# Stick-breaking attention: a backward running sum along the keys in place of products with triangles of ones

## The chip, the cores and the metric

One core of one Trainium2 chip runs the whole program. The metric is device microseconds for one execution. Of the engines, TensorE (PE in the profile, PEld for its weight loads) multiplies, VectorE (DVE) and ScalarE (ACT) work elementwise, GpSimd (POOL) and SyncE (SP) here mostly start transfers.

## What is computed

One layer of a hybrid encoder trunk on 512 frames of width 2048, in float32: RMSNorm, one wide projection, three attention branches A, B and C of 4 heads of width 128 each, SiLU gates, an up-projection per branch, sigmoid merge gates, an output projection and the residual. The change concerns branch C, stick-breaking attention. Cut to what matters, per head and block of 128 queries:

```python
z = q @ k.T * scale                                   # causal blocks of keys
mask = key < query                                    # strictly causal
lk = where(mask, log_sigmoid(-z), 0.0)
r = sum of lk over the keys from this one to the last # a suffix sum along the keys
a = where(mask, exp(z + r), 0.0)
out = a @ v
```

The reference writes the suffix sum as a product with a triangle of ones inside each block of 128 keys, plus the totals of the later blocks.

## The kernel before

**Number format.** Matrix products run in fp32r. To keep float32 accuracy every operand is split into a high part (ScalarE copies it to fp32r, L243) and a low part (VectorE subtracts, L247), and a product is made of high x high, high x low and low x high (`mm3`, L257 to L259).

**Weights.** Nearly all of TensorE's work is the weight products at L262. The weights come in units of 128 x 1024; ScalarE makes `wh`, VectorE makes `wl`, two units ahead of TensorE. From the second half of the start-up on, two output columns are made together by a scheme of seven products (`PairTask`, in the order 1, 2, 6, 5, 7, 3, 4). Each of the seven is a unit of 16 products on TensorE: 8 of 512 columns with `wh`, 8 of 256 columns with `wl`. Between the units VectorE and ScalarE take results out of PSUM and combine them (L703 to L759), and VectorE adds weight tiles (L641, L647).

**Heads.** The twelve heads run in the order C0 to C3, B0 to B3, A0 to A3, each beside the weight products of later columns. Their products use four PSUM tiles `att`; the weight products use others (`acc`). A stick-breaking head (class `Head`, `n == C`) does this:

- `plain` splits q and k.
- `stick_scores(j)`, for the key block j, makes the scores with the keys of the block as rows and the queries from that block on as columns: 512, 384, 256 or 128 columns. ScalarE takes them out (`z`), VectorE and ScalarE make log(1 + exp(z)) in `lk` (L1073 to L1079), VectorE sets it to zero on and above the diagonal (L1080, `m01`), and it is split into `lkh` and `lkl`.
- `stick_sums(j)` sums over keys, which lie on the partitions, on TensorE: for the block j a product with the triangle `nu_r`, for each later block a product with the full matrix `nones_r`, both for the high and the low part (L1096), and a product that adds the mask (L1098). VectorE adds `z` (L1107), ScalarE takes Exp (L1110), and the result, which has the keys on the partitions already, is split into `ah` and `al`.
- `v_trans` transposes v (L1123), `av` multiplies (L1162 to L1164), and `silu` makes the gate.

A softmax head (A, B) has its scores the other way round, queries on the partitions, and turns the weights at the end by transposes (L1025):

```python
def soft_trans(self, j):
    for i in range(QB):
        yield self.event("s", i)
    yield from self.parts_of(j)
    yield atts, 1
    yield PE, 0.11 * (QB - j)
    ps = att()
    for i in range(j, QB):
        nc.tensor.transpose(ps[:, blk(i)], self.p[i][:, blk(j)], identf)
    if self.nth("t", QB):
        give(t2s, 3)
    yield from split(*self.hl[j], ps[:, j * P:], S - j * P, self.event("a", j))
    give(atts)
```

**What sets the order.** Each piece of work is a generator that yields what it waits for (events, free slots of tiles) and which engine it will use for how long by a formula in the code. `Flow` plays these through on three clocks, for TensorE, ScalarE and VectorE, takes the piece that can start first (then the one due first), and calls it; the order in which the pieces are called is the order of the instructions on these three engines. On the chip each engine then works through its own list in order, and waits where an operand is not there. A head's pieces are started at set units (`OFF`: scores from the head's unit + `cs`, sums from + `ct`), and wait for what they need. Slots: 21 tiles of 128 x 512 (`t2s`) for everything, 4 PSUM tiles `att`.

Of the kernel before, what the change touches and what calls it, by code (L numbers as in the profile page):

```python
# [161 lines left out]
def hybrid_kernel(  # L162
# [50 lines left out]
    def blk(i):  # L213
        return slice(i * P, (i + 1) * P)
# [67 lines left out]
    def stored(slots, n, kb):  # L282
# [30 lines left out]

    nc.gpsimd.affine_select(out=nu_f, in_=onef, pattern=[[-1, P]], base=0, channel_multiplier=1,
                            compare_op=ALU.is_ge, fill=0.0)
# [569 lines left out]
    class Head:  # L885
        def __init__(self, n, h, last=False):
            self.n, self.h, self.last = n, h, last
            self.prev = heads[-1] if heads else None
            heads.append(self)
            self.hl, self.z, self.lk = [None] * QB, [None] * QB, [None] * QB  # L890
            self.summed, self.lk_given = [False] * QB, []
            self.c, self.ev, self.count = {}, {}, {}
# [137 lines left out]

        def tile_of(self, key, j, dt=F32):

            self.tiles = getattr(self, "tiles", {})
            if (key, j) not in self.tiles:
                t = t2(key, dt)
                self.tiles[key, j] = t[:, :S - j * P]
                if j in (1, 3):
                    self.tiles[key, 1], self.tiles[key, 3] = t[:, :S - P], t[:, S - P:]
            return self.tiles[key, j]

        def turn(self):
# [4 lines left out]

        def room_of(self, key, j, n):
            if j in (1, 3):
                if (key, 4 - j) in self.count:
                    return  # L1050
            self.count[key, j] = 1
            yield t2s, n

        def stick_scores(self, j):
            n = S - j * P
            for e in (("p", Q), ("p", K)):
                yield self.event(*e)
            yield from self.room_of("z", j, 1)
            yield atts, 1
            (qh, ql), (kh, kl) = self.c[Q], self.c[K]  # L1060
            yield PE, mm_us(n, 3)
            ps = att()[:, j * P:]
# [3 lines left out]
            z = self.z[j] = self.tile_of("z", j)  # L1066
            yield ACT, act_us(n)
            nc.scalar.activation(z, ps, AF.Copy, scale=SCALE)
            give(atts)
            yield t2s, 1  # L1070
            t = t2("lk")[:, j * P:]
            yield DVE, dve_us(n)
            nc.vector.scalar_tensor_tensor(t, z, -1.0, z, op0=ALU.mult, op1=ALU.min)  # L1073
            yield ACT, act_us(n)
            nc.scalar.activation(t, t, AF.Exp)
            yield ACT, act_us(n)
            nc.scalar.activation(t, t, AF.Ln, bias=1.0)
            yield DVE, dve_us(n) + dve_us(P)
            nc.vector.scalar_tensor_tensor(t, z, 0.0, t, op0=ALU.max, op1=ALU.add)  # L1079
            nc.vector.tensor_mul(t[:, :P], t[:, :P], m01)  # L1080
            yield from self.room_of("lk", j, 2)
            self.lk[j] = self.tile_of("lkh", j, F32R), self.tile_of("lkl", j, F32R)
            yield from split(*self.lk[j], t, n, self.event("s", j))
            give(t2s)

        def stick_sums(self, j):
            n = S - j * P
            for i in range(QB):
                yield self.event("s", i)
            yield from self.parts_of(j)  # L1090
            yield atts, 1
            yield PE, sum(mm_us(S - i * P, 2) for i in range(j, QB)) + mm_us(P)
            ps = att()
            for i in range(j, QB):
                for part in self.lk[i]:
                    nc.tensor.matmul(ps[:, i * P:], nu_r if i == j else nones_r, part,  # L1096
                                     start=i == j and part is self.lk[j][0], stop=False)
            nc.tensor.matmul(ps[:, blk(j)], identb, mskc, start=False, stop=True)  # L1098

            self.summed[j] = True  # L1100
            for k, need in ((0, (0,)), (2, (0, 1, 2)), (1, (0, 1, 2, 3))):
                if k not in self.lk_given and all(self.summed[i] for i in need):
                    self.lk_given.append(k)
                    give(t2s, 2)
            a = self.z[j]
            yield DVE, dve_us(n)
            nc.vector.tensor_add(a, a, ps[:, j * P:])  # L1107
            give(atts)
            yield ACT, act_us(n)
            nc.scalar.activation(a, a, AF.Exp)  # L1110
            yield from split(*self.hl[j], a, n, self.event("a", j))
            if self.nth("z", QB):
                give(t2s, 3)

# [61 lines left out]
        def stages(self):  # L1176

            s, t = (OFF["s1"], OFF["t1"]) if self.last else (OFF["s"], OFF["t"])
            v, o = (OFF["v1"], OFF["av1"]) if self.last else (OFF["v"], OFF["av"])
            one = lambda fn, i: lambda: fn(i)  # L1180
            if self.n == C:
                g = [(0, one(self.plain, K)), (0, one(self.plain, Q))]
# [453 lines left out]
```

## Time and profile before

| | |
|---|---|
| Time, three runs | 1356.82, 1358.31, 1358.43 us; median 1358.31 |
| Span of the profiled execution | 1356.7 us |
| Busy: PE, PEld, DVE, ACT, POOL | 98%, 85%, 81%, 59%, 7% of the span |
| Transfers | 262 MB, 193 GB/s on average |
| First products with triangles, last ones | start at 147.4 us, 353.8 us |
| Chain that ended last | 96% PE, of it 82% the products `acc` at L262, 0.8% L1096 |

The profiled execution's own time is not listed beside the three runs; its span is 0.1 us below the quickest of them. A busy share says how much of the time an engine had an instruction in work; matmuls overlap each other, so the share of PE is read together with its list of waits.

### The profile page before, as it was taken

To read this page: it belongs to the slowest core of one execution; us is meant where nothing else is said; L and a number is where in the kernel's file an instruction comes from. 1 tells how busy PE (TensorE), PEld (TensorE's weight loads), DVE (VectorE), ACT (ScalarE), POOL (GpSimd) and SP (SyncE) were. 2 spreads that over 40 slices of the span, in tenths; PEclk is the share of its full clock that TensorE was granted. 3 is DMA by queue.
4 is the path that set the end of the run, shared out by engine and by line. 5 is a ranking of instruction groups with operands and counts; after the bars stand their busy time and mean duration, and the time that the engine had idled before them with its cause. 6 is when DMAs were issued, how large, how long until landed. Compare 5 with 4: busy or idle time off the path is not lost.

```text
span 1356.7 us, 19786 instructions
## 1 busy us (share of the span) xinstructions
PE 1334.7 (98%) x7394; PEld 1157.1 (85%) x7394; DVE 1105.1 (81%) x1592; ACT 802.8 (59%) x1240; POOL 94.2 (7%) x125
## 2 busy tenths in 40 slices
PE   7999999999999999999999999999999999989998
PEld 5788888888888888888888888888888788878887
DVE  5898997978878788787888878778787877888786
ACT  6655765646565566655667556665566655454443
POOL 0000000000100001000010000100000000000100
PEclk9999999999999999999999999999999999989999
DMA  9555667677677777777767777677767755748893
GB/s 328 170 145 151 178 163 197 169 209 192 173 189 204 196 205 172 193 198 200 201 171 196 186 193 201 168 186 199 184 182 248 252 187 181 209 127 246 237 243 95
DMA packets 91056, 262.01 MB, mean 193 GB/s; under 512 B 10168, under 2 KB 16440, under 8 KB 90960
## 3 DMA queue, kind: packets, MB, share of 16 engines
q1 hardware_dynamic: 72384, 201.96, 44.5%
q0 software_dynamic: 14976, 54.53, 24.3%
q10 hardware_dynamic: 3600, 4.26, 0.9%
q8 instruction: 58, 0.95, 0.3%
q14 instruction: 38, 0.31, 0.1%
HBM read 241.03 MB, written 19.69 MB: 192 GB/s over the span
## 4 chain that ended last, share of the span: by engine, by line
PE 96%; DVE 2%; DMA 0%; issue 0%; ACT 0%; SPq 0%; DVEq 0%; ACTq 0%
PE acc L262 82%; PE att L262 8%; DVE wl L247 1%; PE att L1096 1%; PE att L1025 1%; DVE m L247 1%; PE att L1164 1%; PE att L1163 1%; PE att L258 1%; PE att L259 1%; PE att L257 1%; PE att L1162 1%; DMA x<-in_xT 0%; PE att L1123 0%; PE att L923 0%
## 5 line engine op out<-in xcount | busy, mean ns | idle before, releaser
L247 DVE TENSOR_TENSOR wl<-raw,wh 128x1024 fp32r<-128x1024 f32 (+1 forms) x412 | 493.6, 1199 | 156.6 <-ACT wh L243 153.7
L243 ACT ACTIVATE wh<-raw 128x1024 fp32r<-128x1024 f32 (+1 forms) x412 | 427.2, 1038 | 148.6 <-PE acc L262 68.6
L262 PE MATMUL acc<-x,wh 128*128 128x512 f32 x1600 | 417.5, 396 | 9.9 <-ACT wh L243 9.9
L262 PEld LDWEIGHTS acc<-x,wh 128*128 128x128 f32 x1600 | 286.5, 189 | 61.6 <-ACT wh L243 9.9
L262 PE MATMUL acc<-t,wh 128*128 128x512 f32 x1056 | 273.7, 395 | 0.0
L262 PEld LDWEIGHTS acc<-x,wl 128*128 128x128 f32 x1504 | 210.5, 190 | 18.9
L262 PE MATMUL acc<-x,wl 128*128 128x256 f32 (+1 forms) x1504 | 223.6, 289 | 0.0
L262 PEld LDWEIGHTS acc<-t,wh 128*128 128x128 f32 x1056 | 187.5, 189 | 31.3
L262 PEld LDWEIGHTS acc<-t,wl 128*128 128x128 f32 x1056 | 145.1, 190 | 11.1
L262 PE MATMUL acc<-t,wl 128*128 128x256 f32 x1056 | 148.6, 282 | 0.0
L278 POOL DMA_DIRECT2D raw<-in_w_col x88 | 76.0, 864 | 941.0 <-DMA raw<-in_w_col 482.4
L262 PE MATMUL acc<-m,wh 128*128 128x512 f32 x448 | 114.4, 398 | 6.4 <-DVE m L247 6.0
L262 PEld LDWEIGHTS acc<-m,wh 128*128 128x128 f32 x448 | 81.8, 192 | 21.8 <-DVE m L247 6.4
L757 ACT ACTIVATE c<-acc 128x256 f32<-128x256 f32 x50 | 19.2, 383 | 104.2 <-PE acc L262 99.2
L735 ACT ACTIVATE u<-acc 128x512 f32<-128x512 f32 x50 | 29.8, 597 | 73.3 <-PE acc L262 73.3
L262 PE MATMUL att<-y,wh 128*128 128x512 f32 x256 | 66.6, 391 | 1.3 <-DVE y L247 1.3
L262 PEld LDWEIGHTS acc<-m,wl 128*128 128x128 f32 x448 | 62.1, 193 | 5.2 <-DVE wl L247 0.8
L262 PE MATMUL acc<-m,wl 128*128 128x256 f32 x448 | 63.4, 285 | 0.4 <-DVE wl L247 0.4
L641 DVE TENSOR_TENSOR raw<-raw,raw 128x1024 f32<-128x1024 f32 x52 | 63.4, 1219 | 0.4
L647 DVE TENSOR_TENSOR raw<-raw,raw 128x1024 f32<-128x1024 f32 x52 | 63.3, 1218 | 0.3
L718 ACT ACTIVATE v<-acc 128x512 f32<-128x512 f32 x52 | 31.1, 598 | 49.4 <-PE acc L262 46.1
L262 PEld LDWEIGHTS att<-y,wh 128*128 128x128 f32 x256 | 47.9, 188 | 12.2 <-DVE y L247 2.4
(211 smaller groups left out, 1408.9 us busy)
## 6 DMA issues: line engine op xcount, KB each, us to landing
raw<-in_w_col SPq DMA_DIRECT2D x236, 512.0 KB, 4.3
raw<-in_w_col POOLq DMA_DIRECT2D x88, 512.0 KB, 6.1
raw<-in_w_out SPq DMA_DIRECT2D x40, 512.0 KB, 4.5
gl<-c SPq DMA_DIRECT2D x48, 256.0 KB, 2.6
raw<-in_w_up SPq DMA_DIRECT2D x32, 384.0 KB, 3.2
sg<-gl SPq DMA_DIRECT2D x48, 256.0 KB, 4.7
raw<-in_w_out POOLq DMA_DIRECT2D x16, 512.0 KB, 6.2
x<-in_xT SPq DMA_DIRECT2D x16, 256.0 KB, 7.0
```

The lines of the kernel that those rows point to most:

```text
L243: nc.scalar.activation(hi, src, AF.Copy)
L247: nc.vector.tensor_sub(lo, src, f(hi))
L257: nc.tensor.matmul(ps, lh, rh, start=start, stop=False, skip_group_check=more)
L258: nc.tensor.matmul(ps, lh, rl, start=False, stop=False, skip_group_check=more)
L259: nc.tensor.matmul(ps, ll, rh, start=False, stop=stop, skip_group_check=more)
L262: nc.tensor.matmul(ps, w, x, start=start, stop=stop, skip_group_check=more)
L278: nc.gpsimd.dma_start(to, src, accum_op=ALU.add)
L641: nc.vector.tensor_add(w[1], w[1], w[5])
L647: nc.vector.tensor_add(w[2], w[2], w[1])
L718: nc.scalar.activation(self.v, ps, AF.Copy)
L735: nc.scalar.activation(self.u, ps, AF.Copy)
L757: nc.scalar.activation(c, ps[:, RH], AF.Copy, scale=-1.0)
```

## The change

The scores of a stick-breaking head are made with the queries on the partitions, as in a softmax head, so that the keys lie along the row. The mask is added to the scores of the diagonal block (VectorE). log(1 + exp(z)) is made as before. The sum over the later keys is one instruction of VectorE a block of queries, a running sum that starts at the row's end and goes backwards (all operands are `t[:, ::-1]`; the second operation, a maximum with the same values, leaves the sum as it is, since all terms are at least zero). VectorE subtracts it from z, ScalarE takes Exp, and the weights are turned by `soft_trans` and split as in a softmax head. The split of the log terms into high and low parts, the 20 products with triangles and full matrices and the 4 mask products of each head are gone, and with them three constants. A new first piece, `stick_start`, takes three tiles for z after the head before has its own; nine were taken piece by piece before (three for z, six for the split log terms). The diff, cut to its core:

```diff
-    nones_r = cp.tile([P, P], F32R, name="nones_r")
-    nc.vector.tensor_scalar_mul(nones_r, onef, -1.0)
...
-    nu_r = cp.tile([P, P], F32R, name="nu_r")
-    nc.vector.tensor_scalar_mul(nu_r, nu_f, -1.0)
...
-    m01 = cp.tile([P, P], F32, name="m01")
-    nc.gpsimd.affine_select(out=m01, in_=onef, pattern=[[1, P]], base=0, channel_multiplier=-1,
-                            compare_op=ALU.is_gt, fill=0.0)
-    mskc = cp.tile([P, P], BF16, name="mskc")
-    nc.gpsimd.affine_select(out=zerof, in_=zerof, pattern=[[1, P]], base=0, channel_multiplier=-1,
+    mskc = cp.tile([P, P], F32, name="mskc")
+    nc.gpsimd.affine_select(out=mskc, in_=zerof, pattern=[[-1, P]], base=0, channel_multiplier=1,
                             compare_op=ALU.is_gt, fill=NEG)
-    nc.vector.tensor_copy(mskc, zerof)
...
-        def stick_scores(self, j):
-            n = S - j * P
-            for e in (("p", Q), ("p", K)):
+        def stick_start(self):
+            yield from self.turn()
+            yield t2s, 3
+            self.p = tri("p")[::-1]
+            set_(self.event("room"))
+
+        def stick_scores(self, i):
+            m = (i + 1) * P
+            for e in (("p", Q), ("p", K), ("room",)):
                 yield self.event(*e)
-            yield from self.room_of("z", j, 1)
             yield atts, 1
             (qh, ql), (kh, kl) = self.c[Q], self.c[K]
...
-            mm3(ps, kh[:, blk(j)], kl[:, blk(j)], qh[:, j * P:], ql[:, j * P:], True, True)
+            mm3(ps, qh[:, blk(i)], ql[:, blk(i)], kh[:, :m], kl[:, :m], True, True)
...
+            yield DVE, dve_us(P)
+            nc.vector.tensor_add(z[:, blk(i)], z[:, blk(i)], mskc)
...
             nc.vector.scalar_tensor_tensor(t, z, 0.0, t, op0=ALU.max, op1=ALU.add)
-            nc.vector.tensor_mul(t[:, :P], t[:, :P], m01)
-            yield from self.room_of("lk", j, 2)
-            self.lk[j] = self.tile_of("lkh", j, F32R), self.tile_of("lkl", j, F32R)
-            yield from split(*self.lk[j], t, n, self.event("s", j))
+            yield DVE, dve_us(2 * m)
+            back = t[:, ::-1]
+            nc.vector.tensor_tensor_scan(back, back, back, 0.0, op0=ALU.add, op1=ALU.max)
+            yield DVE, dve_us(m)
+            nc.vector.tensor_sub(z, z, t)
             give(t2s)
-
-        def stick_sums(self, j):
...
+            yield ACT, act_us(m)
+            nc.scalar.activation(z, z, AF.Exp)
+            set_(self.event("s", i))
...
-                g += [(OFF["cs"] + i, one(self.stick_scores, QB - 1 - i)) for i in range(QB)]
-                g += [(OFF["ct"] + i, one(self.stick_sums, i)) for i in range(QB)]
+                g = [(0, one(self.plain, K)), (0, one(self.plain, Q)), (OFF["cs"] - 1, self.stick_start)]
+                g += [(OFF["cs"] + i, one(self.stick_scores, i)) for i in range(QB)]
+                g += [(OFF["ct"] + i, one(self.soft_trans, i)) for i in range(QB)]
```

**Where the instructions stand now.** TensorE, the fourth stick-breaking head (C3). Before, its first group of sums, in the middle of a unit of weight products (`acc` are weight products, `att` the head's):

```order
L262 MATMUL acc_3379<-x_12_144,wh_3377 128x512
L1096 MATMUL att_3443<-lkh_3386,nu_r 128x512
L1096 MATMUL att_3443<-lkl_3387,nu_r 128x512
L1096 MATMUL att_3443<-lkh_3232,nones_r 128x384
L1096 MATMUL att_3443<-lkl_3233,nones_r 128x384
L1096 MATMUL att_3443<-lkh_3291,nones_r 128x256
L1096 MATMUL att_3443<-lkl_3292,nones_r 128x256
L1096 MATMUL att_3443<-lkh_3232,nones_r 128x128
L1096 MATMUL att_3443<-lkl_3233,nones_r 128x128
L1098 LDWEIGHTS identb
L1098 MATMUL att_3443<-mskc,identb 128x128
L262 MATMUL acc_3379<-x_13_145,wh_3377 128x512
```

Three more such groups follow, one in each of the next three units. In the changed program (L1013 is the line of the transposes there) the head's transposes stand in the unit after the next two, nine in a row, the tenth 14 products on:

```order
L262 MATMUL acc_3397<-x_6_130,wh_3343 128x512
L1013 MATMUL att_3412<-identf,p_3042 128x128
L1013 MATMUL att_3412<-identf,p_3043 128x128
L1013 MATMUL att_3412<-identf,p_3042 128x128
L1013 MATMUL att_3412<-identf,p_3041 128x128
L1013 MATMUL att_3418<-identf,p_3043 128x128
L1013 MATMUL att_3418<-identf,p_3042 128x128
L1013 MATMUL att_3418<-identf,p_3041 128x128
L1013 MATMUL att_3423<-identf,p_3042 128x128
L1013 MATMUL att_3423<-identf,p_3041 128x128
L262 MATMUL acc_3397<-x_7_131,wh_3343 128x512
```

What moved: four groups over four units became one block, behind the Exp of the last block of queries. In the first two heads all ten stand in a row; the first head's transposes are 30 weight products later than its last sums were, and the second head's four score groups, which stood between 26 and 64 products after those sums, stand together 51 products after those transposes. From the second head on the products with v keep their places, and behind the fourth head the order on all engines is the same as before.

VectorE, the same head, the stretch between the results of the second and the seventh of a group's weight units (L727 and L739; the order names the tiles: u and v are those results, lk the log terms, z the scores). Before:

```order
L727 TENSOR_TENSOR u_3317<-u_3317,acc_3320 128x512
L703 TENSOR_TENSOR c_553_3361<-u_3317 128x256
L247 TENSOR_TENSOR wl_3348<-raw_3135,wh_3347 128x1024
L1079 SCALAR_TENSOR_TENSOR lk_3271<-z_3262,lk_3271 128x512
L1080 TENSOR_TENSOR lk_3271<-lk_3271,m_104 128x128
L247 TENSOR_TENSOR lkl_3233<-lk_3236,lkh_3232 128x384
L247 TENSOR_TENSOR wl_3378<-raw_3114,wh_3377 128x1024
L247 TENSOR_TENSOR lkl_3387<-lk_3271,lkh_3386 128x512
L247 TENSOR_TENSOR wl_3409<-raw_3168,wh_3408 128x1024
L739 TENSOR_TENSOR v_3407<-v_3407,acc_3287 128x512
```

And in the changed program, where L716 and L728 are those two lines, p holds the scores, L1057 is the old L1079, L1060 the running sum (the order's view names it by its family, SCALAR_TENSOR_TENSOR) and L1062 the subtraction:

```order
L716 TENSOR_TENSOR u_3230<-u_3230,acc_3233 128x512
L692 TENSOR_TENSOR c_531_3270<-u_3230 128x256
L1051 SCALAR_TENSOR_TENSOR lk_3224<-p_3041 128x512
L247 TENSOR_TENSOR wl_3264<-raw_3058,wh_3263 128x1024
L1062 TENSOR_TENSOR p_3043<-p_3043,lk_3138 128x256
L1057 SCALAR_TENSOR_TENSOR lk_3191<-p_3042,lk_3191 128x384
L1057 SCALAR_TENSOR_TENSOR lk_3224<-p_3041,lk_3224 128x512
L1060 SCALAR_TENSOR_TENSOR lk_3191<-lk_3191 128x384
L247 TENSOR_TENSOR wl_3292<-raw_3034,wh_3291 128x1024
L1060 SCALAR_TENSOR_TENSOR lk_3224<-lk_3224 128x512
L247 TENSOR_TENSOR wl_3320<-raw_3089,wh_3319 128x1024
L728 TENSOR_TENSOR v_3318<-v_3318,acc_3203 128x512
```

What moved: six operations of the head stand in the stretch where four stood, the running sums of 384 and 512 columns among them (L1051 is the old L1073); the next line that takes a result, L737 in the changed program, comes four rows later, and behind it L692 and the subtraction of 512 columns, on which Exp and the transposes wait.

More of the change, by code (lines that the diff above doesn't have):

```diff
@@ L889, in __init__ @@
             heads.append(self)
-            self.hl, self.z, self.lk = [None] * QB, [None] * QB, [None] * QB
-            self.summed, self.lk_given = [False] * QB, []
+            self.hl = [None] * QB
             self.c, self.ev, self.count = {}, {}, {}
@@ L1029, in soft_trans @@
             give(atts)
[L1031 to L1039, printed above, removed]
         def turn(self):
@@ L1045, in turn @@
                     yield self.prev.event("hl", j)
[L1047 to L1052, printed above, removed]
-        def stick_scores(self, j):
-            n = S - j * P
-            for e in (("p", Q), ("p", K)):
+        def stick_start(self):
[3 more added lines that the diff above has]
+            set_(self.event("room"))
@@ L1057, in stick_scores @@
+        def stick_scores(self, i):
+            m = (i + 1) * P
+            for e in (("p", Q), ("p", K), ("room",)):
                 yield self.event(*e)
-            yield from self.room_of("z", j, 1)
             yield atts, 1
             (qh, ql), (kh, kl) = self.c[Q], self.c[K]
-            yield PE, mm_us(n, 3)
-            ps = att()[:, j * P:]
-            mm3(ps, kh[:, blk(j)], kl[:, blk(j)], qh[:, j * P:], ql[:, j * P:], True, True)
+            yield PE, mm_us(m, 3)
+            ps = att()[:, :m]
+            mm3(ps, qh[:, blk(i)], ql[:, blk(i)], kh[:, :m], kl[:, :m], True, True)
@@ L1064, in stick_scores @@
             if self.nth("s", QB):
                 give(t2s, 4)
-            z = self.z[j] = self.tile_of("z", j)
-            yield ACT, act_us(n)
+            z = self.p[i]
+            yield ACT, act_us(m)
             nc.scalar.activation(z, ps, AF.Copy, scale=SCALE)
             give(atts)
+            yield DVE, dve_us(P)
+            nc.vector.tensor_add(z[:, blk(i)], z[:, blk(i)], mskc)
             yield t2s, 1
-            t = t2("lk")[:, j * P:]
-            yield DVE, dve_us(n)
+            t = t2("lk")[:, :m]
@@ L1073, in stick_scores @@
+            yield DVE, dve_us(m)
             nc.vector.scalar_tensor_tensor(t, z, -1.0, z, op0=ALU.mult, op1=ALU.min)
-            yield ACT, act_us(n)
+            yield ACT, act_us(m)
             nc.scalar.activation(t, t, AF.Exp)
-            yield ACT, act_us(n)
+            yield ACT, act_us(m)
             nc.scalar.activation(t, t, AF.Ln, bias=1.0)
-            yield DVE, dve_us(n) + dve_us(P)
+            yield DVE, dve_us(m)
             nc.vector.scalar_tensor_tensor(t, z, 0.0, t, op0=ALU.max, op1=ALU.add)
-            nc.vector.tensor_mul(t[:, :P], t[:, :P], m01)
@@ L1081, in stick_scores @@
-            yield from self.room_of("lk", j, 2)
-            self.lk[j] = self.tile_of("lkh", j, F32R), self.tile_of("lkl", j, F32R)
-            yield from split(*self.lk[j], t, n, self.event("s", j))
-            give(t2s)
-        def stick_sums(self, j):
[L1087 to L1113, printed above, removed]
@@ L1115, in v_trans @@
+            yield DVE, dve_us(2 * m)
+            back = t[:, ::-1]
+            nc.vector.tensor_tensor_scan(back, back, back, 0.0, op0=ALU.add, op1=ALU.max)
+            yield DVE, dve_us(m)
+            nc.vector.tensor_sub(z, z, t)
+            give(t2s)
+            yield ACT, act_us(m)
+            nc.scalar.activation(z, z, AF.Exp)
+            set_(self.event("s", i))
         def v_trans(self):
@@ L1181, in stages @@
             if self.n == C:
-                g = [(0, one(self.plain, K)), (0, one(self.plain, Q))]
-                g += [(OFF["cs"] + i, one(self.stick_scores, QB - 1 - i)) for i in range(QB)]
-                g += [(OFF["ct"] + i, one(self.stick_sums, i)) for i in range(QB)]
+                g = [(0, one(self.plain, K)), (0, one(self.plain, Q)), (OFF["cs"] - 1, self.stick_start)]
+                g += [(OFF["cs"] + i, one(self.stick_scores, i)) for i in range(QB)]
+                g += [(OFF["ct"] + i, one(self.soft_trans, i)) for i in range(QB)]
             else:
```

2 lines of the change are left out of this document (removed).

## Prediction

> **What bounds the kernel now.** I began with the page's share of each engine, then asked what TensorE waited for, then looked at the stretch in which the stick-breaking heads run.
>
> ```profile
> span 1356.7 us, 19786 instructions
> PE 1334.7 (98%) x7394; PEld 1157.1 (85%) x7394; DVE 1105.1 (81%) x1592; ACT 802.8 (59%) x1240; POOL 94.2 (7%) x125
> ```
>
> The waits of TensorE (reason, total us, times, longest) are these and no others:
>
> ```profile
> PE acc L262 <- ACT wh L243: 10.3, 2, 9.9
> PE acc L262 <- DVE m L247: 6.0, 1, 6.0
> PE att L262 <- DVE y L247: 1.3, 2, 1.0
> PE acc L262 <- DVE wl L247: 0.4, 1, 0.4
> ```
>
> The 9.9 us is the wait for the first weights at the start; tiles m and y belong to the up-projection and the output, behind all heads. The busy time by stages, in the stretch of the last stick-breaking head (columns: stretch, length and PE busy, PEld, DVE, ACT, POOL, clock, DMA share, GB/s):
>
> ```profile
> 280.00:360.00 80.00, 80.00 (x470) 70.87 (x469) 66.51 (x92) 45.30 (x71) 6.04 (x7) 1.00 0.72 188
> ```
>
> TensorE is busy for all 80 us at a granted clock of 1.00, and nothing in the list of waits lies here. So in this stretch its instruction stream is the time: a product taken out of it brings the next weight product forward, as long as VectorE (66.5 of 80 us), ScalarE (45.3) and the DMA engines (0.72) keep up. A busy share alone would not prove that, since matmuls overlap; the missing waits do.
>
> **What the change removes on TensorE.** In each stick-breaking head the 20 products with triangles (L1096) and 4 mask products (L1098) go. I price them by starts, not by durations, because neighbours overlap: from the first one's start to the start of what follows. The fourth head's four groups, in TensorE's timeline (start, length, what):
>
> ```profile
> 342.60 0.39 PE L1096 MATMUL att<-lkh,nu_r 128*128 128x512 f32 x1
> ...
> 343.86 0.71 PE L262 MATMUL acc<-x,wh 128*128 128x512 f32 x2
> ...
> 346.75 0.34 PE L1096 MATMUL att<-lkh,nu_r 128*128 128x384 f32 x1
> ...
> 347.54 0.71 PE L262 MATMUL acc<-t,wh 128*128 128x512 f32 x2
> ...
> 350.43 0.28 PE L1096 MATMUL att<-lkh,nu_r 128*128 128x256 f32 x1
> ...
> 350.87 0.94 PE L262 MATMUL acc<-x,wh 128*128 128x512 f32 x3
> ...
> 353.76 0.22 PE L1096 MATMUL att<-lkh,nu_r 128*128 128x128 f32 x1
> ...
> 354.00 0.61 PE L1123 MATMUL att<-identf,c 128*128 128x128 f32 x4
> ```
>
> 343.86 - 342.60 = 1.26; 347.54 - 346.75 = 0.79; 350.87 - 350.43 = 0.44; 354.00 - 353.76 = 0.24. That is 2.73 us a head. The four heads issue the same products, so 4 x 2.73 = 10.92 us leave the stream.
>
> **What it adds on TensorE.** Ten transposes of 128 x 128 a head. The softmax heads do the same transposes now (L1025), in groups of four, three and one in these rows:
>
> ```profile
> 443.00 0.60 PE L1025 MATMUL att<-identf,p 128*128 128x128 f32 x4
> 443.35 0.71 PE L262 MATMUL acc<-x,wh 128*128 128x512 f32 x2
> ...
> 446.25 0.49 PE L1025 MATMUL att<-identf,p 128*128 128x128 f32 x3
> 446.50 0.94 PE L262 MATMUL acc<-t,wh 128*128 128x512 f32 x3
> ...
> 452.86 0.27 PE L1025 MATMUL att<-identf,p 128*128 128x128 f32 x1
> 452.89 1.17 PE L262 MATMUL acc<-t,wh 128*128 128x512 f32 x4
> ```
>
> A group of four takes 0.35 us, of three 0.25, of one 0.03: every further transpose costs (0.35 - 0.03) / 3 = 0.107. The order of the changed program puts ten in a row in the first two heads and nine plus one in the last two. Ten: 0.03 + 9 x 0.107 = 0.99. Nine and one: 0.03 + 8 x 0.107 + 0.03 = 0.92. Together 2 x 0.99 + 2 x 0.92 = 3.82 us.
>
> One transpose lasts 0.27 us in these rows, and that length would tell otherwise: 40 x 0.27 = 10.8 us, as much as is removed. The Trainium skill bears on this (TensorE: Matmul & The Clock Gate, Part 4: PE-mode transpose): it gives about 275 ns for a transpose inside a kernel, says that access latency makes up most of it, and that transposes do not count as work for the full clock. An estimate by that page, each transpose paid in full, is 40 x 0.275 = 11.0 us and no gain. The trace agrees with the length (0.27) and not with paying it: four start within 0.35 us, at a clock that the stages show as 1.00. I take the starts.
>
> **The sum.** 10.92 - 3.82 = 7.1 us less on TensorE. The score products keep their widths (512, 384, 256, 128, three each), with the roles of q and k swapped: nothing. Three constants on VectorE and some on GpSimd at the start go: hidden under the 9.9 us that the first product waits for its weights. Behind the fourth head's last transpose the order of all engines is that of before, so the rest shifts as a whole. The profiled span is 1356.7; the three runs are 1356.82 to 1358.43, so this execution was one of the quick ones, by 1.6 us from the median. 1358.31 - 7.1 = **1351.2**.
>
> **What must hide: VectorE and ScalarE.** Rows of operations that come or go (ns: least, median, most; a head has one of each width):
>
> ```profile
> L854 DVE TENSOR_TENSOR_SCAN fs<-fu,fv x1: 1217/1217/1217, 704.8 to 704.8; 128x512 f32<-128x512 f32 x1
> L247 DVE TENSOR_TENSOR lkl<-lk,lkh x16: 281/484/686, 131.8 to 339.2; 128x128 fp32r<-128x128 f32 x4, 128x256 fp32r<-128x256 f32 x4, 128x384 fp32r<-128x384 f32 x4, 128x512 fp32r<-128x512 f32 x4
> L243 ACT ACTIVATE lkh<-lk x16: 299/458/633, 126.6 to 338.0; 128x128 fp32r<-128x128 f32 x4, 128x256 fp32r<-128x256 f32 x4, 128x384 fp32r<-128x384 f32 x4, 128x512 fp32r<-128x512 f32 x4
> ```
>
> The subtractions cost 281 ns at 128 and 686 at 512 columns, so 146 fixed and 1.05 a column. A scan with the same fixed part is 1217 = 146 + 512 x 2.09; that makes 414, 682, 949 and 1217 ns, 3.26 us a head. The four subtractions lkl go (4 x 0.484 = 1.94), the final subtraction of sums replaces the addition from PSUM, and four mask additions replace four mask products of the same 128 columns. VectorE: +1.3 us a head, against 13.5 us idle in the 80 shown. ScalarE: 4 x 0.458 = 1.8 us less. On average both fit.
>
> The tightest place is local. In the fourth head the order has, from L716 to L728 of the changed program, eleven VectorE operations, all inside three units of weight products, and then the chain L737, L692, subtraction of 512, Exp on ScalarE, transposes. VectorE's handover and a short chain in the present timeline, and an Exp of that size:
>
> ```profile
> 146.92 0.69 DVE L748 TENSOR_TENSOR u<-u,acc 128x512 f32<-128x512 f32 x1
> 147.64 0.42 DVE L703 TENSOR_TENSOR c<-u 128x256 f32<-128x256 f32 x1
> 147.98 1.22 DVE L641 TENSOR_TENSOR raw<-raw,raw 128x1024 f32<-128x1024 f32 x1
> 149.12 1.22 DVE L247 TENSOR_TENSOR wl<-raw,wh 128x1024 fp32r<-128x1024 f32 x1
> ...
> 152.30 0.62 ACT L1110 ACTIVATE z<-z 128x512 f32<-128x512 f32 x1
> ```
>
> By lengths the eleven are 0.69 + 0.42 + 0.69 + 1.22 + 0.42 + 0.55 + 0.69 + 0.95 + 1.22 + 1.22 + 1.22 = 9.3 us (0.55 and 0.95 are the two formulas at 384 columns); each next one starts about 0.08 before the last has ended (147.98 + 1.22 - 149.12), so 8.4. A unit of 16 weight products lasted 346.75 - 343.86 = 2.89; three are 8.7. VectorE is just full there, with 0.3 to spare. After it the transposes stand 16 + 5 products behind the unit whose end frees L737: 2.89 + 5 x 0.23 = 4.0 us (0.23 is the step of the 512-wide products: 0.94 for three against 0.71 for two). The chain needs about 0.2 + 0.72 + 0.34 + 0.69 + 0.62 = 2.6, where 0.2 is my allowance for the release. So 1.4 us are free before TensorE would wait. If VectorE ran later than that, TensorE would stand at the first transpose, and everything behind it in its stream (the next weight products) with it.
>
> No row shows a scan whose operands run backwards. The nearest is the forward one above; a plain subtraction, 0.69, bounds it below, and for a bound above I take four times the forward one. I take the forward price, since the same operation on the same number of elements is the nearest row. The Trainium skill (Vector Engine (DVE) Microarchitecture Reference, section 5.1 Performance modes) lists an operand with a negative step among the things not measured; no run here shows it yet.
>
> **The rivals.**
> - *VectorE a little late.* Two of the scans (949 and 1217) lie in the tight stretch, 2.17 us. At twice the price VectorE would be 2.17 later, less 1.4 free: 0.8 us of waiting a head, 3.1 in all: 1351.2 + 3.1 = 1354.3. For it: VectorE is just full there. Against: TensorE has not waited for VectorE once in these heads.
> - *VectorE sets the pace: slower.* The same place and mechanism, with the backward scan at four times the price: 3 x 2.17 - 1.4 = 5.1 us a head, 20.4 in all, 1358.3 - 7.1 + 20.4 = 1371.6. It turns into a loss where the wait exceeds 7.1 / 4 = 1.8 a head, so from a price of 1 + (1.8 + 1.4) / 2.17 = 2.5 times the forward one. For it: nothing but the missing row.
> - *Transposes cost their length.* 40 x 0.27 = 10.8 against 10.92: 1358.2. Against: the starts above.
> - *Something else paces the stretch.* If weights arrived only just in time, TensorE would wait for wh for what it saved: 1358.3. Against: DMA share 0.72 and no such wait behind the start.
>
> **How the numbers follow.** My forecast gets 0.78, the slightly late VectorE 0.09, transposes at full length 0.06, another pace 0.03, the loss 0.04. A measurement of this kernel can tell about 0.2% from no change, 2.7 us, so "faster" begins at 1355.6: 0.78 + 0.09 = 0.87. Same: 0.06 + 0.03 = 0.09. Slower: 0.04. Low end: with the transposes in blocks as cheap as in the small groups of a softmax head (0.35 + 0.25 + 0.03, and about 0.14 for the pair: 0.77 a head) the gain is 10.92 - 3.1 = 7.8, and with about 1 us for the spread of the runs 1349.5. High end: the late VectorE at 1354.3 with 0.7 of that spread, 1355.0.
>
> **What would show it.** Right: TensorE still without waits between 120 and 1000 us; the first weight product after the fourth head's transposes about 7 us earlier in its order than now; ten transposes in about 1.0 us; a backward scan of 512 near 1.2 us. Wrong: a row in which a transpose of p waits for the Exp of p, scans well above 1.2 us, or TensorE's stream unchanged in length because transposes start 0.27 us apart.

## The result and the profile after

The changed kernel takes 1351.01 us (median of five runs, 1350.72 to 1351.68) against 1358.22 of five runs before (1356.82 to 1358.43). The two medians lie 7.2 us apart. The ratio on record is 0.9954, 95% interval 0.9943 to 0.9965: about 6.2 us less, between 4.8 and 7.7. The profiled execution of after is the one of 1351.01; its span is 7.4 us shorter than that of before. The time of an execution is about 1.7 us more than its span (1351.01 against 1349.3).

The page's first rows of after:

```profile
span 1349.3 us, 19660 instructions
PE 1326.0 (98%) x7338; PEld 1149.2 (85%) x7338; DVE 1108.8 (82%) x1589; ACT 797.3 (59%) x1224; POOL 93.5 (7%) x123
```

TensorE's busy time fell by 8.7, VectorE's rose by 3.7, ScalarE's fell by 5.5. As before TensorE fills 98% of the span, so the question is again where its stream got shorter, and whether it waits. Its waits in after (reason, total us, times, longest):

```profile
PE acc L262 <- ACT wh L243: 10.6, 3, 10.0
PE acc L262 <- DVE m L247: 6.0, 1, 6.0
PE att L262 <- DVE y L247: 1.3, 2, 1.0
PE att L1013 <- ACT p L1065: 1.0, 1, 1.0
PE acc L262 <- DVE wl L247: 0.4, 1, 0.4
```

One row is new: once, 1.0 us long, the transposes of the weights (L1013 in after) wait for the Exp of p. And wh has a third, short wait. The stretches with the four stick-breaking heads (columns as in the prediction):

```profile
120.00:200.00 80.00, 79.79 (x465) 70.42 (x465) 76.71 (x129) 50.33 (x82) 6.86 (x8) 1.00 0.72 181
200.00:280.00 80.00, 79.01 (x465) 69.56 (x464) 69.92 (x97) 48.41 (x76) 6.04 (x7) 1.00 0.68 187
280.00:360.00 80.00, 80.00 (x466) 70.59 (x465) 66.69 (x91) 46.68 (x70) 6.91 (x8) 1.00 0.72 191
```

The new waits lie in the first two stretches, 0.21 and 0.99; the last one has none. VectorE is fullest in the first, 76.71 of 80. The prediction had shown only the last stretch, the emptiest of the three for VectorE in after.

The new instructions at work, in the timeline of TensorE and ScalarE around the third head's transposes, and the scans of the two kinds (L1060 backward, L843 forward; ns least, median, most):

```profile
258.33 0.63 ACT L1065 ACTIVATE p<-p 128x512 f32<-128x512 f32 x1 [1.40 <-DVE p L1062]
...
260.30 1.15 PE L1013 MATMUL att<-identf,p 128*128 128x128 f32 x9
261.20 0.94 PE L262 MATMUL acc<-x,wh 128*128 128x512 f32 x3
```

```profile
L1060 DVE TENSOR_TENSOR_SCAN lk<-lk x16: 417/812/1220, 130.8 to 335.2; 128x128 f32<-128x128 f32 x4, 128x256 f32<-128x256 f32 x4, 128x384 f32<-128x384 f32 x4, 128x512 f32<-128x512 f32 x4
...
L843 DVE TENSOR_TENSOR_SCAN fs<-fu,fv x1: 1219/1219/1219, 698.1 to 698.1; 128x512 f32<-128x512 f32 x1
```

Nine transposes took 261.20 - 260.30 = 0.90 us (0.03 + 8 x 0.107 = 0.89 was forecast), and the backward scan of 512 took 1220 ns against 1219 of the forward one: running backwards costs nothing. The instruction order of all engines is the same again from shortly behind the fourth head, so the start of one product there, in both traces, says what the heads gave. First before, then after (the product at 349.89; the row above it is used further down):

```profile
356.55 2.00 PE L262 MATMUL acc<-t,wh 128*128 128x512 f32 x8
```

```profile
346.53 0.86 PE L262 MATMUL acc<-x,wh 128*128 128x512 f32 x3
...
349.89 2.00 PE L262 MATMUL acc<-t,wh 128*128 128x512 f32 x8
```

This product starts 6.66 us earlier. Counting weight products through both timelines tells where that comes from: 0.61 up to the 20th product, long before the first head; 2.21 in the first two heads; 1.93 in the third; 1.93 in the fourth. The heads together gave 6.1. Behind them the distance stays at 6.7 for 4300 products, and near 1207 us it grows to 7.4.

**The stall of the second head.** TensorE, VectorE and ScalarE in after's timeline (the value in brackets is the idle time before, and what ended it):

```profile
194.87 1.22 DVE L1060 TENSOR_TENSOR_SCAN lk<-lk 128x512 f32<-128x512 f32 x1
...
198.01 1.11 PE L262 MATMUL acc<-x,wl 128*128 128x256 f32 x8
...
199.16 0.69 DVE L716 TENSOR_TENSOR u<-u,acc 128x512 f32<-128x512 f32 x1
199.33 2.12 PE L262 MATMUL acc<-t,wh 128*128 128x512 f32 x8 [0.21 <-ACT wh L243]
200.23 1.22 DVE L636 TENSOR_TENSOR raw<-raw,raw 128x1024 f32<-128x1024 f32 x1
201.28 0.49 PE L1013 MATMUL att<-identf,p 128*128 128x128 f32 x3
201.37 0.68 DVE L1062 TENSOR_TENSOR p<-p,lk 128x512 f32<-128x512 f32 x1
202.08 0.63 ACT L1065 ACTIVATE p<-p 128x512 f32<-128x512 f32 x1 [1.85 <-DVE p L1062]
202.76 0.98 PE L1013 MATMUL att<-identf,p 128*128 128x128 f32 x7 [0.99 <-ACT p L1065]
```

The transposes of the three narrow blocks run, then TensorE stands 0.99 us for the fourth. Its p comes late, and ScalarE stood idle 1.85 us for it, because the subtraction at 201.37 stands in VectorE's queue behind L716 and the weight sum L636. The scan of 512 had ended at 194.87 + 1.22 = 196.09, five us before. L716 takes the result of the unit that TensorE ended at 198.01 + 1.11 = 199.12, so it could hardly have started before 199.16, however little VectorE had had to do until then. What made `wh` late by 0.21 is not traced further.

**The parts before and behind the heads.** At the start, the first weight products step at about half speed: 0.43 instead of 0.23 us from one to the next. Rows of before, then of after:

```profile
14.29 1.05 PE L262 MATMUL acc<-x,wh 128*128 128x512 f32 x2
15.15 0.97 PE L262 MATMUL att<-x,wh 128*128 128x512 f32 x2
15.96 0.39 PE L262 MATMUL att<-x,w 128*8 128x512 f32 x1
```

```profile
14.40 0.67 PE L262 MATMUL acc<-x,wh 128*128 128x512 f32 x2
14.90 0.63 PE L262 MATMUL att<-x,wh 128*128 128x512 f32 x2
```

Before, the pairs at 14.29 and 15.15 take 0.86 and 0.81 to the next start; in after the pairs at 14.40 and 14.90 take 0.50 and 0.47. That is 0.7, less the 0.1 by which after began later. Behind the 6.0 us wait for m something alike gives 0.7: eight products that take 1.84 us elsewhere took 3.41 there before and 2.76 in after. Neither belongs to the changed instructions: runs 1 and 3 below have after's instructions up to the heads and 0.6 and 0.4 us more at the start, runs 2 and 7 have 0.6 and 0.7 more than after near 1207 us. So of the 7.4 us between the two spans 6.1 come from the heads, which is near the 6.2 of the ratio.

### The profile page after: what moved, and what is told of

Read it like the earlier page. It is cut to its first block, busy times and chain, and to the rows that moved or that the text cites. A ratio compares the mean times of both kernels' runs of the same rounds, so it can differ in the third digit from the quotient of the medians.

```text
span 1349.3 us, 19660 instructions
## 1 busy us (share of the span) xinstructions
PE 1326.0 (98%) x7338; PEld 1149.2 (85%) x7338; DVE 1108.8 (82%) x1589; ACT 797.3 (59%) x1224; POOL 93.5 (7%) x123
## 4 chain that ended last, share of the span: by engine, by line
PE 96%; DVE 3%; DMA 0%; issue 0%; ACT 0%; SPq 0%; DVEq 0%; ACTq 0%
PE acc L262 82%; PE att L262 8%; PE att L1013 1%; DVE wl L247 1%; DVE m L247 1%; PE att L1116 1%; PE att L258 1%; PE att L1117 1%; PE att L259 1%; PE att L257 1%; PE att L1115 1%; DMA x<-in_xT 0%; PE att L1076 0%; PE att L911 0%; PE att L912 0%
## 5 line engine op out<-in xcount | busy, mean ns | idle before, releaser
L746 ACT ACTIVATE c<-acc 128x256 f32<-128x256 f32 x50 | 19.2, 384 | 105.4 <-PE acc L262 100.4
L636 DVE TENSOR_TENSOR raw<-raw,raw 128x1024 f32<-128x1024 f32 x52 | 63.5, 1221 | 0.4
L630 DVE TENSOR_TENSOR raw<-raw,raw 128x1024 f32<-128x1024 f32 x52 | 63.4, 1220 | 0.4
```

The source lines that it names most:

```text
L630: nc.vector.tensor_add(w[1], w[1], w[5])
L636: nc.vector.tensor_add(w[2], w[2], w[1])
L746: nc.scalar.activation(c, ps[:, RH], AF.Copy, scale=-1.0)
```

## The experiments

All times are medians with their least and greatest; ratios are against the kernel before, run on the same chip beside it. "Above after" is against the 1351.01 of the first measurement. "Heads" is the distance gained or lost between the 560th and the 1700th weight product, which leaves out the half-speed products of the start.

**1. Each transpose twice.** In the stick-breaking heads alone:

```diff
-                nc.tensor.transpose(ps[:, blk(i)], self.p[i][:, blk(j)], identf)
+                for _ in range(2 if self.n == C else 1):
+                    nc.tensor.transpose(ps[:, blk(i)], self.p[i][:, blk(j)], identf)
```

> The changed kernel, but each of the 40 transposes of stick-breaking heads is issued twice in a row; nothing else moves. If a transpose costs its step in TensorE's stream (0.107 us, from groups of four and one), 40 x 0.107 = 4.3 us more than the changed kernel's 1351.0: 1355.3, and ten become twenty in about 2.1 us. If it costs its length (0.27 us), 40 x 0.27 = 10.8 us more: 1361.8. If TensorE's stream is not what sets the time here: 1351.0.

Measured 1354.73 us (1354.06 to 1355.70), ratio 0.9981 (0.9971 to 0.9990), 3.7 above after; heads +4.1 against after. Its fourth head:

```profile
347.47 2.13 PE L1014 MATMUL att<-identf,p 128*128 128x128 f32 x18
349.36 0.95 PE L262 MATMUL acc<-x,wh 128*128 128x512 f32 x3
```

Eighteen took 1.89, nine more than after's nine cost 0.99: 0.11 each. Forty transposes more cost 4.1, not 40 x 0.27 = 10.8. That transposes are paid by their step is shown, and the rival that they cost their length is refuted.

**2. Before, without most of the triangle products.** Of each block's products with triangles the first alone is left (4 of 20 a head); everything else is as before, the splits on ScalarE and VectorE too:

```diff
-            for i in range(j, QB):
-                for part in self.lk[i]:
-                    nc.tensor.matmul(ps[:, i * P:], nu_r if i == j else nones_r, part,
-                                     start=i == j and part is self.lk[j][0], stop=False)
+            nc.tensor.matmul(ps[:, j * P:], nu_r, self.lk[j][0], start=True, stop=False)
```

> The kernel before, in which each group of sums issues only its first product (triangle, high part) and the mask; the other 16 products of a head are left out, so the sums are incomplete, and nothing else moves. This is the removal alone. If TensorE's stream sets the time, a head's 2.73 us fall to about 0.65 (steps 0.23, 0.17, 0.11, 0.06 and four masks), so 4 x 2.1 = 8.3 us less than before: 1349.9. If the weights' arrival or VectorE sets the pace: 1358.2, with new waits of the weight products for wh or wl.

Measured 1350.57 us (1349.71 to 1351.34), ratio 0.9949 (0.9934 to 0.9964), against 1357.51 of before beside it; heads -6.8 against before, with one new wait of 0.8 for the low part of q and k. Without that wait they would have given 7.6, of 8.3 expected. What leaves TensorE's stream here is paid back nearly in full: nothing else paces the stretch.

**3. Each backward scan twice.**

```diff
-            nc.vector.tensor_tensor_scan(back, back, back, 0.0, op0=ALU.add, op1=ALU.max)
+            for _ in range(2):
+                nc.vector.tensor_tensor_scan(back, back, back, 0.0, op0=ALU.add, op1=ALU.max)
```

> The changed kernel, but each running sum is issued twice in a row on VectorE (so the sums are sums of sums); the order is unchanged. By the account of the tight stretch, the third and fourth head's transposes wait (2.17 - 1.4) = 0.8 us each; the second head's transposes, which already wait 1.0 us, wait about 2 us longer; the first head's not at all: 3.6 us more than 1351.0: 1354.6. If VectorE had room everywhere: 1351.0. If VectorE set the pace of the whole stretch: 4 x 3.26 = 13 us more: 1364.

Measured 1359.38 us (1358.53 to 1360.54), ratio 1.0014 (1.0005 to 1.0024): 8.4 above after (heads +8.1) and no gain left. The expectation was 5 us too low. The waits:

```profile
PE acc L262 <- ACT wh L243: 12.8, 3, 9.8
...
PE acc L262 <- DVE v L728: 2.5, 2, 1.3
...
PE acc L262 <- DVE wl L247: 1.2, 2, 0.8
PE att L1013 <- ACT p L1066: 1.0, 1, 1.0
```

The wait for p has not grown at all. What is late is the work queued behind the scans on VectorE: L728, which takes the seventh product's result out of the PSUM that the fourth goes on in, and the weights. With 0.9 for the low part of the attention weights (`al`) the new waits add up to 6.4 of the 8.1; the rest is not traced. The order is that of after, so the room in front of the transposes (1.4 us) was the wrong one to look at.

**4. Each backward scan four times** (the same edit with `range(4)`).

> The changed kernel, but each running sum is issued four times in a row. The prediction's rival on the slower side put such a scan at 5.1 us of waiting in a head; with 5.1 in the third and fourth, about 6.5 in the second, and 3 in the first head 20 us more than 1351.0: 1371, and so slower than before, with TensorE waiting at transposes of p for Exp. If the lateness spreads to the weights' low parts as well, the wait shows at the weight products for wl and the time is nearer to 4 x 3 x 3.26 = 39 us more: 1390. If VectorE's idle time takes it up: under 1355.

Measured 1392.99 us (1391.12 to 1393.33), ratio 1.0259 (1.0243 to 1.0274): 42 above after. The slower rival had said 20 above, from the transposes alone. The other branch of the expectation, 1390 with waits for the weights, is near in size, but the largest wait is one that it did not name, for L728. The waits, one stretch of the heads, and what follows the longest kind of wait in TensorE's timeline:

```profile
PE acc L262 <- DVE v L728: 16.6, 4, 5.5
PE acc L262 <- ACT wh L243: 14.4, 3, 10.1
PE acc L262 <- DVE wl L247: 6.1, 5, 2.2
```

```profile
120.00:200.00 80.00, 73.72 (x407) 64.39 (x406) 76.46 (x129) 44.61 (x74) 6.00 (x7) 0.94 0.63 159
```

```profile
151.36 3.75 PE L262 MATMUL acc<-t,wh 128*128 128x512 f32 x8 [4.34 <-DVE v L728]
154.91 1.56 PE L262 MATMUL acc<-t,wl 128*128 128x256 f32 x8
156.31 2.00 PE L262 MATMUL acc<-x,wh 128*128 128x512 f32 x8
158.15 1.11 PE L262 MATMUL acc<-x,wl 128*128 128x256 f32 x8
```

After 4.34 us of waiting, eight products take 154.91 - 151.36 = 3.55 us; the same eight take 158.15 - 156.31 = 1.84 a unit later. So this wait costs about two us more in slow products (with those of the eight of 256 columns behind them), and the granted clock of the stretch falls to 0.94.

**5. The transposes later.** The plan reckons the weights of a block 1.5 us later, so the transposes, and the splits behind them, move back (the second head's transposes from behind the 904th weight product to behind the 914th):

```diff
-            set_(self.event("s", i))
+            self.event("s", i).t = flow.fin + 1.5
```

> The changed kernel, but the plan takes a block of weights as ready 1.5 us after its Exp, so that the transposes stand 6 to 10 weight products later in TensorE's order; the work is the same. If the second head's transposes wait because they stand too early, the wait of 1.0 us for Exp goes and the 0.2 us for wh stays: about 1350.0. If what is late there are the weights' parts, TensorE waits for those instead: 1351.0.

Measured 1352.34 us (1350.68 to 1352.45), ratio 0.9961 (0.9947 to 0.9974); heads +0.9 against after. The wait for p is gone, and this row has grown from 0.4 in its place:

```profile
PE acc L262 <- DVE wl L247: 2.1, 2, 1.7
```

So moving the transposes back does not end the second head's stall. The subtraction and the next `wl` still stand behind L716 and L636 on VectorE, and if TensorE does not meet that at p, it meets it at the weights.

**6. The mask as a product.** The mask is added to the scores by a bfloat16 product of 128 columns, as before, and VectorE's four additions a head go (about 1.1 us):

```diff
...
-            mm3(ps, qh[:, blk(i)], ql[:, blk(i)], kh[:, :m], kl[:, :m], True, True)
+            mm3(ps, qh[:, blk(i)], ql[:, blk(i)], kh[:, :m], kl[:, :m], True, False)
+            nc.tensor.matmul(ps[:, blk(i)], identb, mskc, start=False, stop=True)
...
-            yield DVE, dve_us(P)
-            nc.vector.tensor_add(z[:, blk(i)], z[:, blk(i)], mskc)
```

> The changed kernel, but the mask is added by a product with the identity in the scores' group (as in the softmax heads with a mask) and not by VectorE. VectorE has 4 x 0.29 = 1.2 us less a head, TensorE 16 products more at 0.04 us a step, 0.6 us in all. If VectorE's load is what makes the second head's transposes late, the wait of 1.0 us and that of 0.2 for wh go: 1351.0 - 1.2 + 0.6 = 1350.4. If the place in the order makes them late: 1351.6.

Measured 1350.62 us (1350.23 to 1351.51), ratio 0.9955 (0.9942 to 0.9967): no gain over after. TensorE is busy through the stretches in which it stood before:

```profile
120.00:200.00 80.00, 80.00 (x469) 70.04 (x469) 76.31 (x122) 50.06 (x83) 6.87 (x8) 1.00 0.70 180
200.00:280.00 80.00, 80.00 (x473) 70.36 (x473) 67.61 (x93) 47.86 (x76) 6.04 (x7) 1.00 0.72 190
```

The 1.2 us of waits are gone, though the second head's transposes stand three products earlier than in after. The mask products took all of that back. The first ones stand behind the 483rd weight product, so the heads are counted here from the 400th: +0.15 against after, and each head's four mask products put the stream back by 0.46 or 0.47. The expectation had 0.04 for one; they cost 0.12, since the weight product behind one steps 0.31 instead of 0.23.

VectorE's order changed with its load. The last subtraction of the second head, behind L636 in after, stands here ahead of that weight sum (L637 in this run; L717 is L716):

```profile
196.08 0.69 DVE L1062 TENSOR_TENSOR p<-p,lk 128x512 f32<-128x512 f32 x1
196.69 1.22 DVE L637 TENSOR_TENSOR raw<-raw,raw 128x1024 f32<-128x1024 f32 x1
...
200.09 0.68 DVE L717 TENSOR_TENSOR u<-u,acc 128x512 f32<-128x512 f32 x1
```

**7. |z| on ScalarE.** VectorE's minimum of -z and z becomes an Abs on ScalarE, with the sign in the Exp:

```diff
-            yield DVE, dve_us(m)
-            nc.vector.scalar_tensor_tensor(t, z, -1.0, z, op0=ALU.mult, op1=ALU.min)
             yield ACT, act_us(m)
-            nc.scalar.activation(t, t, AF.Exp)
+            nc.scalar.activation(t, z, AF.Abs)
+            yield ACT, act_us(m)
+            nc.scalar.activation(t, t, AF.Exp, scale=-1.0)
```

> The changed kernel, with |z| made by ScalarE (Abs, then Exp with scale -1) instead of by VectorE's minimum of -z and z: four operations a head, about 1.94 us, leave VectorE, and about 1.83 us are added to ScalarE, which is busy about 0.6 of the time. Nothing changes on TensorE. My theory: the waits of the second head (1.0 for p, about 0.2 for wh) come from VectorE being a little too full there; with 1.94 us less they go, the span comes to about 1348.1 and the median to about 1350.0. Rival: the waits have another cause (ScalarE's Exp, the release of the buffers); then they stay, 1351.0, or grow with ScalarE's load.

**8. The changed kernel again**, beside it:

> The changed kernel as it is, once more, beside the other two on the same chip. Every theory expects 1351.0 within the spread of the runs (1350.7 to 1351.7), with the waits for p (1.0) and wh (about 0.2) in the second head again, and the half-speed products at the start ending at another moment by some tenths of a us.

Run 8 measured 1351.13 us (1350.04 to 1352.14), ratio 0.9953 (0.9941 to 0.9966), with the same waits of 1.0 and 0.2. Run 7 measured 1349.39 us (1349.26 to 1349.82), ratio 0.9941 (0.9927 to 0.9954): no run of it is as slow as the quickest of run 8, and the medians lie 1.7 apart. It beats both kernels. Its span is 1348.1, and the list of TensorE's waits is that of the kernel before, row for row and to the tenth: nothing waits in the heads. VectorE is no emptier for it just before the place of the stall: between 180 and 200 us it is busy 19.53 of 20 us here, 19.60 in run 6 and 19.19 in after. Its order moved again: the second head's last subtraction starts at 189.99, ahead of both weight sums.

With less work planned on VectorE the transposes also move forward in the order and fall apart into smaller groups, 7 + 2 + 1 in the first two heads and 4 + 3 + 2 + 1 in the last two. The first head's:

```profile
150.07 0.93 PE L1013 MATMUL att<-identf,p 128*128 128x128 f32 x7
150.76 0.70 PE L262 MATMUL acc<-x,wh 128*128 128x512 f32 x2
...
153.39 0.38 PE L1013 MATMUL att<-identf,p 128*128 128x128 f32 x2
153.52 1.39 PE L262 MATMUL acc<-x,wh 128*128 128x512 f32 x5
...
156.41 0.27 PE L1013 MATMUL att<-identf,p 128*128 128x128 f32 x1
156.43 1.40 PE L262 MATMUL acc<-t,wh 128*128 128x512 f32 x5
```

0.69 + 0.13 + 0.02 = 0.84 us here; the last two heads, by the rows quoted in the prediction and the 0.13 of this pair, 0.35 + 0.25 + 0.13 + 0.03 = 0.76. By the prediction's own method the heads should give 10.92 - 2 x 0.84 - 2 x 0.76 = 7.7 us against before. The trace of run 7 gives 7.7 there.

**9. |z| on ScalarE, and each scan twice.** The edits of 7 and 3 together; the order of the engines is that of run 7 but for the second scans.

> The run with |z| on ScalarE, and each backward scan done twice (sums of sums, so the weights differ). Against the changed kernel VectorE has 3.26 - 1.94 = 1.3 us more a head; against the run with scans done twice alone it has 1.94 less. My theory, that the total load of VectorE in these heads sets the lateness: in proportion to that run's 8.4 us for 3.26 a head, about 3.4 us above the changed kernel, 1354.4. If only the length of the scans themselves in the tight chain counts, 1359.4 as with the scans twice alone.

Measured 1357.53 us (1356.67 to 1359.28), ratio 1.0001 (0.9993 to 1.0010): 6.5 above after, neither 3.4 nor 8.4. Both expectations fell. The wait for p has grown here, unlike in run 3:

```profile
PE att L1013 <- ACT p L1066: 3.4, 2, 1.7
PE acc L262 <- DVE v L728: 2.8, 2, 1.9
```

Run 9 is better compared with run 7, whose order it has: the second scans cost 8.1 us there (1357.53 - 1349.39), nearly as much as the 8.4 in after's order (by the heads alone 7.7 and 8.1). Taking 1.9 us a head off VectorE left little more room for longer scans. The likely reason, which no run isolates, is that the plan, which knows the prices of these operations, had spent it on earlier transposes. I had reckoned with a load and forgotten that the order is made anew for it.

## Why the prediction was right, and where not

- **TensorE's stream sets the time of these stretches: right.** Run 2 takes products out and gets nearly all of them back. No other pace appeared.
- **The sum, 10.92 removed and 3.82 added: right to about a tenth of a us a head.** Nine transposes took 0.90 and ten 1.01 where nothing was late, and in run 7, where nothing waits, the method gives the measured 7.7. The third and fourth head gave 1.93 each against 1.81 forecast. Most of that lies behind the groups: the first weight product behind a group takes 0.08 more (three products 0.94 us at 261.20, three others 0.86 at 346.53), which a price up to the next start leaves out; before has four such places a head there and after three.
- **The hit on the median: partly luck.** The median came out at 1351.0 against 1351.2, though the heads gave 6.1 and not 7.1. The median of 1358.31 that I subtracted from was itself high: beside the experiments, before measured 1357.51, 1356.99 and 1357.45. The two errors nearly cancel. In the profiled pair the half-speed products at the start and near 1207 us, which I had not reckoned with, gave 1.3. I also misread the profiled execution of before as a quick one, by comparing its span with times: with the 1.7 between the two, its 1356.7 is a time of about 1358.4. The forecast did not use that.
- **"VectorE hides it": failed in one head of four.** The sign that I had named for being wrong, a transpose of p that waits for Exp, appeared once. The first two heads gave 2.21 together against 3.48 forecast, and the second head's waits, 0.99 and 0.21, are nearly all of that difference. I had tested the tightest place of the fourth head and taken it for all. In the trace the third head has what I forecast: the Exp ends at 258.33 + 0.63 = 258.96 and the transposes begin at 260.30, 1.3 us free against 1.4. In the second head the subtraction stands behind L716 and L636 on VectorE, as the timeline shows. That the place of the transposes alone is not at fault is shown by run 5, where moving them only moves the wait. In runs 6 and 7, with work taken off VectorE, the wait ends; but there the plan also put the subtraction ahead of the weight sum, and VectorE was just as full up to 200 us. So VectorE's queue is what made p late; whether less work in an unchanged order would have been enough, no run tests.
- **Backward scan at the forward price: right,** 1220 against 1219 ns. The Trainium skill had no figure for a negative step (Vector Engine (DVE) Microarchitecture Reference, section 5.1 Performance modes); in these runs it costs nothing.
- **Transposes at their full length: refuted** by run 1. An estimate by the Trainium skill's 275 ns (TensorE: Matmul & The Clock Gate, Part 4: PE-mode transpose) had given no gain; the length agrees, but one behind another they step 0.11 us.
- **The rivals with a dear scan: mechanism right, place and size wrong.** Twice the price was to cost 3.1 us in all and cost 8.4; four times was to cost 20 and cost 42. The turning point to a loss lies below twice the forward price and not at 2.5 times (an estimate: with 6.1 of gain in the heads and 8.1 lost by the second scans, a straight line gives 1 + 6.1 / 8.1 = 1.75). The step that failed is the 1.4 us of room: it is the room before the transposes, while L728 and the weights stand in the same queue with less. My own count had only 0.3 to spare in front of L728, and I did not carry it into the rivals; with 2.17 us of scans added there, run 3 has two waits of up to 1.3 for it. In run 4, besides, waits of four us and more are followed by products at half speed. The chance of 0.04 for a loss leaned on a reserve that was not there; the price alone, which was right, carried it.
- **The start constants: nothing seen.** The first products of before and after start within 0.1 us of each other (9.86 and 9.96).

Open stays what sets the moment at which the half-speed products end; no run here varies that alone.

## What to carry to other kernels

Where an engine's list of waits is empty over a stretch, price what enters and leaves its stream by the steps from start to start in rows of the same kind; a matmul's own length says little. When such a change loads another engine, go through its queue in every head and not in the one that is easiest to read, and at each place where the first engine waits for it ask what stands ahead: results of the first engine itself, and the weights of the next unit too. The busy share of a stretch does not tell (19.2 of 20 us with the wait, 19.5 without). Where a planner orders the work, taking load off an engine also changes its order; here longer scans, which the plan did not know of, cost nearly as much in either order.

## What the runs showed of the hardware

- A scan along the row with reversed operands costs what the forward one costs: 417 ns at 128 columns, 1220 at 512, about 2.1 ns a column.
- Transposes of 128 x 128 in a row start 0.11 us apart (eighteen in 1.89 us), at a granted clock of 1.00.
- A wait of 4.3 us was followed by eight products in 3.55 us instead of 1.84. Shorter waits do not tell alike: after 1.3 and 2.5 us (run 3) and 1.7 and 1.9 us (run 9) the products stepped 0.24 to 0.25, nearly as usual, but behind waits of 2.0 and 2.2 us in run 4 eight took 2.82 and 2.76. The length of the wait alone does not decide.
- The first 512-wide weight product behind a group of a head's products steps 0.31 us instead of 0.23 (before, after and run 6).
- Between kernels that issue the same instructions there, the half-speed products cost amounts that differ by up to 0.9 us at the start and by up to 1.0 us behind the 6.0 us wait near 1200 us; two executions of the changed kernel agreed within 0.2. For a change of some tenths of a per cent it is worth taking spans apart by a landmark in front of the change and one behind it.
